# A two-layer hybrid decoder on one core: the second layer's split weights made in the first layer's later blocks

## The chip, the cores and the metric

The kernel runs on 1 core of a Trainium2 chip. The core has a matmul engine (PE, with its weight loads, PEld), VectorE (DVE), ScalarE (ACT), GpSimd (POOL), and SyncE (SP), whose instruction stream issues all DMAs of this kernel, one after the other. Each engine runs its own instructions in order. The metric is the device time of one execution in microseconds (us).

## The reference, cut to what matters

Two layers work on 2048 prompt tokens (and on 64 sample tokens: 8 sequences of 8). One input projection feeds four recurrences, whose outputs are gated, joined and projected; cross-attention into 256 memory tokens follows.

```python
def mixer(h, l, pos, st, v_first, P):
    proj = h @ P['w_in'][l]                       # 1024 -> 3920 columns
    p_ret, p_hgrn, p_gla, p_rwkv = jnp.split(proj, [...], axis=-1)
    ...                                           # four chunked recurrences, each gated with silu(g)
    out = jnp.concatenate([o_ret, o_hgrn, o_gla, o_rwkv], axis=-1) @ P['w_out'][l]

def run_trunk(x, pos0, mem_k, mem_v, init, P):
    for l in range(DEPTH):                        # DEPTH = 2
        out, st_l, v_first = mixer(rmsnorm(x, P['norm_mix'][l]), l, pos, ...)
        x = x + out
        x = x + cross_attend(rmsnorm(x, P['norm_x'][l]), P['wq_x'][l], P['wo_x'][l], mem_k[l], mem_v[l])
```

Everything is float32.

## The kernel before, in words

**Blocks.** The prompt is cut into four blocks of 512 tokens; the program goes through the four blocks of the first layer (A0 to A3 below) and then the four of the second (B0 to B3). A block runs: input projections of RWKV, the RWKV recurrence (`R_rwkv`, four 128-token units on two PSUM lanes), projections and recurrence of GLA, of HGRN and of retention (`R_ret`, two halves), the gates (`gates`), and `finish`, with the output projection `w_out`, the next block's norm (`ahead`, `pre_norm`) and cross-attention. The sample tokens ride along: their projections in block 0, most of their recurrences and their gates in blocks 0 and 1, their output in block 1 (`TURN`).

**Split weights.** A product in float32 is made of three faster ones: weight and activation are each split into a rounded half `hi` and the rest `lo` (type fp32r), and hi.hi, hi.lo and lo.hi are added in PSUM (`dense_c`, `dense_t`). The weights of a layer come in 43 pieces of 128 x 1024 numbers (one is smaller): 31 of `w_in`, 8 of `w_out`, 2 of `wq`, 2 of `wo`. The first time that a piece is needed, which is block 0 of its layer, `parts_of` (line 363) loads the raw piece, ScalarE copies it to `hi` (line 358), GpSimd subtracts to get `lo` (line 359, recorded as L236), and both are stored to DRAM as `parted[key]`; later blocks load the stored pair, 1 MB. `plain` keeps the raw piece as well: the sample tokens' products read it (`wraw`, in float32).

**Buffers.** Raw pieces use the pool `wrp` (3 buffers, tag `w`), pairs the pool `whp` (3 buffers: `whl`). Dense products go to the two PSUM banks `psd`; `psa` and `psc` serve two lanes of the recurrences, `psb` a third.

**What sets the order.** The program is written block by block, and a scheduler then orders each engine's instructions: by priority (the place in the program, shifted by `rank` with the table `PRI`), among those that it takes to be ready by its own estimate of times. So an instruction can stand far from where it is written. At run time each engine keeps that order.

**Names in rows.** `xs` is a normed row block of the next block, transposed on PE (`psb<-fpack,xs`, line 272); `osb` is a recurrence's output in `head_norm` (lines 550 to 569), transposed when its norm is done; `S_ret` and `dn_rv` belong to retention; `th` is a gate's evacuation from `psd` (lines 1265 to 1267); `ol` the `lo` half of a gated output (line 1477).

Of the kernel before, what the change touches and what calls it, by code (L numbers as in the profile page):

```python
# [142 lines left out]
def decoder(ctx, tc, I, C, O):  # L143
# [43 lines left out]
    def right(name):  # L187
        return sided(name, "right")
# [23 lines left out]
    @contextmanager  # L212
    def on_lane(x):
        old, lane[0] = lane[0], x
        yield
        lane[0] = old
# [146 lines left out]
    def parts_of(key, hl, raw, load, plain, again):  # L363


        made = key in parted
        x = None
        if plain or not made:
            x = raw()
            load(x)  # L370
        if made:
            dma(hl.bitcast(F32), parted[key])
        else:
            split_w(x, hl)
            if again:
                parted[key] = drp.tile(list(hl.shape), F32, name="w_" + "_".join(map(str, key)))
                dma(parted[key], hl.bitcast(F32))
        return x

    def load_c(pieces, key, plain, again=True):  # L380

# [890 lines left out]
    def block(l, b, act, hts, st, smp, on, ons, ds, op):  # L1272
# [101 lines left out]
        qk = op.tile([128, 2, TB], F32, name="dn_qk", tag="on_hgrn")  # L1374
        qks = T("ds_qk", [128, 2, SN]) if smp else None
        for i, nm in enumerate(("gla_q", "gla_k")):
            with within("gla", i, 4):
                proj_c(nm, 0, lambda ps: copy_ps(qk[:, i, :], ps), lambda ps: copy_ps(qks[:, i, :], ps))
        gv = op.tile([128, NT, 256], F32, name="dn_gv", tag="on_ret")
        gvs = T("ds_gv", [128, 2, SN]) if smp else None  # L1380
        with within("gla", 2, 4):
            proj_t("gla_v", lambda ps, t0: copy_ps(gv[:, t0:t0 + 2, :], ps), gvs)
        for hb in range(2):
            with within("wk2", hb, 2), on_lane("b"), right("wk2") as wp:
                R_gla(l, pr, st["gla"], dict(qk=h2(qk, hb), v=t2(gv, hb), sm=sm[:, hb * 256:(hb + 1) * 256]), h2(on["gla"], hb), wp)
        if smp:
# [37 lines left out]
        with within("hg", 4, 6):  # L1424
            proj_t("hg_i", lambda ps, t0: copy_ps(hv[:, t0:t0 + 2, :], ps), hvs)
        for hb in range(2):
            with within("wk3", hb, 2), on_lane("b"), right("wk3") as wp:
                R_hgrn(l, pr, st["hgrn"], dict(q=h2(hq, hb), f=h2(hf, hb), v=t2(hv, hb)), h2(on["hgrn"], hb), wp)

# [9 lines left out]
        with within("ret", 2, 3):  # L1439
            proj_t("ret_v", lambda ps, t0: copy_ps(rq["v"][:, t0:t0 + 2, :], ps), rqs["v"])  # L1440
        for hb in range(2):
            with left("wk4") as wp:
                R_ret(l, pr, st["ret"], {nm: t2(rq[nm], hb) for nm in "qkv"}, h2(on["ret"], hb), wp)
        if smp:
# [3 lines left out]
    def gates(l, act, hts, st, smp, on, ons, proj_c, op, wp):  # L1448

        c = cols[l]  # L1450
        hi = [wp.tile([128, 2, 2, TB], F32R, name="oh", tag=f"oh{j}") for j in range(2)]
        oT = [None] * 4
        for nm, cn in (("rwkv", "rw_g"), ("gla", "gla_g"), ("hgrn", "hg_g"), ("ret", "ret_g")):
            h = OKEY.index(nm)
            val = []
            for i in range(2):
                def ev(ps):
                    g = ps
                    if nm == "rwkv":
                        g = dnp.tile([128, TB], F32, name="gs", tag="gs")  # L1460
                        shift_mix(ps, 7 + i, c, st["carry"], g)
                    th = dnp.tile([128, TB], F32, name="th", tag="th", bufs=2)
                    gate_mul(th, g, on[nm][:, i, :], th)
                    A.activation(hi[h // 2][:, h % 2, i, :], th, AF.Copy)
                    val.append(th)

                def evs(ps):
                    g = ps
                    if nm == "rwkv":
                        g = dnp.tile([128, TB], F32, name="gs", tag="gs")[:, :SN]  # L1470
                        shift_mix_s(ps, 7 + i, c, st["shs"], st["ssh"], g)
                    th = dnp.tile([128, SN], F32, name="ths", tag="ths")
                    gate_mul(th, g, ons[nm][:, i, :], ons[nm][:, i, :])
                proj_c(cn, i * 128, ev, evs, smp, hts)
            lo = op.tile([128, 2, TB], F32R, name="ol", tag="on_" + nm)
            for i in range(2):
                tt(V, lo[:, i, :], val[i], hi[h // 2][:, h % 2, i, :].bitcast(F32), ALU.subtract)
            oT[h] = (hi[h // 2][:, h % 2], lo)
        return oT
# [400 lines left out]
        shift_rows(so, O[11][l], SB)  # L1880

    steps = [(l, b) for l in range(depth) for b in range(NB)]
    st = mem = nxt = None
    with on_lane("b"), right("wkn") as wp:
        nxt = []
# [12 lines left out]
    for i, (l, b) in enumerate(steps):  # L1898
        act, hts = nxt
        smp = b == 0  # L1900
        if b == 0:
            ons = {nm: dnp.tile([128, 2, SN], F32, name="ons_" + nm, tag="ons_" + nm) for nm in OKEY}
            ds, hts_l = {}, hts
        fin = b == TURN["end"][l == depth - 1]
        with left("on") as op:
# [9 lines left out]
            rank("D_gate")  # L1915
            oT = gates(l, act, hts_l, st, b == TURN["gate"], on, ons, proj_c, op, wf)
            if b == NB - 1:
                with on_lane("b"), right("wko") as wp:
                    layer_out(l, st, wp)
                    if l + 1 < depth:  # L1920
                        st = layer_state(l + 1, wp)
# [100 lines left out]
```

## Time and profile before

| | us |
|---|---|
| three runs, median (lowest to highest) | 3608.89 (3601.26 to 3626.65) |
| profiled execution, own time | 3606.38 |
| its span, first to last instruction | 3604.6 |
| blocks A1, A2 | 418.1, 427.5 |
| blocks B0, B1, B2 | 518.8, 444.1, 435.4 |

A block is measured from the ScalarE evacuation of its first projection (`sm`, line 536) to that of the next block. Busy times of an engine in a stretch are read against its length; PEclk is the granted clock of PE as a share of the full 2.4 GHz (half of it is the lower level, 1.2 GHz), and its mean over a stretch lies between. In a timeline row the bracket at the end is the time that the engine stood idle before it, and what released it.

### The profile page before, as it was taken

Reading aid. Unit: us, or ns where it says so; the run is one execution under the profiler, and the core shown is the slowest. Engines: PE = TensorE matmul, PEld = TensorE weight load, DVE = VectorE, ACT = ScalarE, POOL = GpSimd, SP = SyncE. Lnnn points to the kernel's source line nnn. Section 1 sums busy time; section 2 is a strip of 40 time slices with the busy share of each in tenths; the row PEclk is TensorE's granted clock in tenths of the full one; section 3 lists DMA queues with packets and bytes.
Section 4 is the critical chain, followed back from the end, with each engine's and each line's share of the span. In section 5 each row is a group of like instructions: output and inputs, shape, how many; then the busy total and the mean of one; then the engine's idle time right before and its main releaser. Section 6 shows DMA issues by size and latency. Waiting matters only on the chain.

```text
span 3604.6 us, 88705 instructions
## 1 busy us (share of the span) xinstructions
PE 3396.8 (94%) x36362; PEld 2817.2 (78%) x36362; DVE 2280.4 (63%) x7543; ACT 1392.1 (39%) x3489; POOL 561.4 (16%) x760
## 2 busy tenths in 40 slices
PE   7999999999999999999999999999889999999998
PEld 5767787777877888788877778778777778877887
DVE  4677645876337754786457865468744677547754
ACT  4452334522244324532445433453214442354323
POOL 3323331020000100110122233101200011000100
PEclk9998999999999999999999999999989999999999
DMA  6432675236652254324542348531554522542254
GB/s 190 151 107 81 187 242 193 72 100 202 212 200 72 100 192 148 113 87 171 180 159 83 103 137 267 172 132 66 160 189 167 170 86 94 193 172 86 73 199 184
DMA packets 244156, 530.92 MB, mean 147 GB/s; under 512 B 66983, under 2 KB 181927, under 8 KB 199719
## 3 DMA queue, kind: packets, MB, share of 16 engines
q1 hardware_dynamic: 243750, 525.25, 42.8%
q8 instruction: 287, 4.70, 0.5%
q14 instruction: 119, 0.97, 0.1%
HBM read 410.04 MB, written 115.16 MB: 146 GB/s over the span
## 4 chain that ended last, share of the span: by engine, by line
PE 73%; DVE 14%; ACT 5%; issue 4%; DMA 2%; POOL 1%; SPq 0%; ACTq 0%; POOLq 0%; DVEq 0%
PE psd L230 40%; PE psc L230 12%; PE psa L230 10%; PE psb L230 5%; PE psc L272 2%; PE psa L272 2%; PE psb L272 2%; DVE rsq L236 1%; DVE Wb L937 1%; DMA wraw<-in_w_in 1%; ACT Xb L939 1%; DVE hri L292 1%; DVE sT L745 1%; DVE hss L561 1%; DVE osb L236 0%
## 5 line engine op out<-in xcount | busy, mean ns | idle before, releaser
L230 PE MATMUL psd<-act,whl 128*128 128x512 f32 (+1 forms) x4032 | 1020.3, 405 | 22.7 <-DVE th L1266 9.6
L230 PEld LDWEIGHTS psd<-act,whl 128*128 128x128 f32 (+1 forms) x4032 | 751.6, 191 | 199.4 <-issue 17.4
L230 PE MATMUL psd<-whl,act 128*128 128x256 f32 x3840 | 544.7, 293 | 5.2 <-POOL whl L236 3.4
L230 PEld LDWEIGHTS psd<-whl,act 128*128 128x128 f32 x3840 | 485.9, 194 | 27.4 <-issue 9.8
L236 POOL TENSOR_TENSOR whl<-wraw,whl 128x1024 fp32r<-128x1024 f32 (+1 forms) x90 | 218.2, 2429 | 335.3 <-ACT whl L358 303.6
L230 PE MATMUL psd<-whl,oh 128*128 128x256 f32 x1152 | 211.6, 284 | 1.2 <-DMA whl<-w_w_out 1.2
L280 POOL TENSOR_TENSOR ri<-ri,mhalf 128x1 f32<-128x1 f32 (+1 forms) x87 | 49.2, 566 | 1039.4 <-DVE ri L279 1005.5
L230 PEld LDWEIGHTS psd<-whl,oh 128*128 128x128 f32 x1152 | 177.5, 189 | 2.6 <-DMA whl<-w_w_out 0.9
L230 PE MATMUL psd<-whl,ol 128*128 128x256 f32 x576 | 162.8, 283 | 0.0
L939 ACT ACTIVATE Xb<-X 32x128 f32<-32x128 f32 x324 | 99.1, 306 | 126.0 <-DVE X L955 78.1
L358 ACT ACTIVATE whl<-wraw 128x1024 fp32r<-128x1024 f32 (+1 forms) x90 | 94.1, 1049 | 124.4 <-PE psa L230 42.4
L745 DVE COPY_PREDICATED sT<-upack,psb 128x128 f32<-128x128 uint8 x320 | 92.6, 326 | 33.1 <-PE psb L230 29.5
L236 DVE TENSOR_TENSOR x<-x,psd 128x256 f32<-128x256 f32 x72 | 30.3, 421 | 128.3 <-PE psd L230 128.3
L230 PEld LDWEIGHTS psd<-whl,ol 128*128 128x128 f32 x576 | 108.6, 189 | 0.4 <-DVE ol L236 0.4
L230 PE MATMUL psb<-dn_hq,dn_hf 64*64 64x32 f32 (+1 forms) x3840 | 99.9, 225 | 7.8 <-DVE dn_hq L236 5.0
L230 PEld LDWEIGHTS psb<-dn_hq,dn_hf 64*64 64x64 f32 x3840 | 82.4, 137 | 31.0 <-issue 17.9
L435 ACT ACTIVATE xs<-xn 128x1024 f32<-128x1024 f32 (+1 forms) x34 | 35.8, 1054 | 155.4 <-PE psb L272 151.2
L1266 DVE SCALAR_TENSOR_TENSOR th<-th,psd 128x512 f32<-128x512 f32 x48 | 32.4, 686 | 91.8 <-ACT th L1265 91.8
L230 PE MATMUL psd<-hts,wraw 128*64 128x64 f32 x1984 | 84.1, 229 | 3.4 <-DVE th L1266 3.4
L230 PEld LDWEIGHTS psd<-hts,wraw 128*64 128x64 f32 x1984 | 69.9, 139 | 21.4 <-issue 11.0
L230 PE MATMUL psa<-whl,oh 128*128 128x256 f32 x448 | 82.8, 283 | 0.0
L230 PE MATMUL psc<-whl,oh 128*128 128x256 f32 x448 | 82.7, 283 | 0.0
(760 smaller groups left out, 7302.3 us busy)
## 6 DMA issues: line engine op xcount, KB each, us to landing
whl<-w_w_out SPq DMA_DIRECT2D x56, 1024.0 KB
wraw<-in_w_in SPq DMA_DIRECT2D x76, 512.0 KB
wraw<-in_w_out SPq DMA_DIRECT2D x32, 512.0 KB
w_w_out<-whl SPq DMA_DIRECT2D x16, 1024.0 KB
x<-x SPq DMA_DIRECT2D x32, 512.0 KB
whl<-w_rw_r SPq DMA_DIRECT2D x12, 1024.0 KB
whl<-w_rw_k SPq DMA_DIRECT2D x12, 1024.0 KB
whl<-w_rw_v SPq DMA_DIRECT2D x12, 1024.0 KB
```

The source lines that it names most:

```text
L230: PE.matmul(out, lhsT=lhsT, rhs=rhs, start=start, stop=stop, skip_group_check=True)
L236: e.tensor_tensor(out, a, b, op)
L272: PE.transpose(out, in_, ident[:rows, :rows])
L280: G.tensor_tensor(y, y, mhalf[:P], ALU.pow)
L292: V.scalar_tensor_tensor(y, t, 1.5, y, ALU.add, ALU.mult)
L358: A.activation(hl[:, 0], raw, AF.Copy)
L435: A.activation(out, xt, AF.Square, accum_out=ss[:P])
L561: V.tensor_reduce(ss[:P, :n4], sq[:P, :n4], AX.X, ALU.add)
L745: V.copy_predicated(out, bc(mk, [P, w, 32 // s, s]), ps)
L937: V.tensor_copy(o, i)
L939: A.activation(o, i, AF.Copy)
L1266: V.scalar_tensor_tensor(th, th, 1.0, x, ALU.add, ALU.mult)
```

## The change

The second layer's 43 pieces are no longer split by `parts_of` in B0. A generator, `prepare(l)`, makes one piece at a time: it loads the raw piece into a `wrp` buffer `lo`, ScalarE copies it to a second `wrp` buffer `hi`, GpSimd subtracts in place, and two DMAs store the halves in DRAM. `some(n)` advances it by n pieces; the calls are written into A1 to A3 (up to 16 pieces in each block: at the GLA projections, before each recurrence half of GLA, HGRN and retention, and at the gates). Since `parted` then holds every key, B0 loads pairs, as the later blocks do, and raw pieces only where the sample tokens need them.

```diff
--- before.py
+++ after.py
@@ -376,6 +376,46 @@
                 parted[key] = drp.tile(list(hl.shape), F32, name="w_" + "_".join(map(str, key)))
                 dma(parted[key], hl.bitcast(F32))
         return x
+
+    def prepare(l):
+
+        w = I["w_in"][l]
+        col = lambda nm, o, n: w[:, OFF[nm] + o:OFF[nm] + o + n]
+        rows = lambda ap: ap.rearrange("(k p) n -> p k n", p=128)
+        half = lambda ap, h: rows(ap[h * 512:(h + 1) * 512])
+        todo = [((l, "low"), [128, 8, 80], [(rows(col(nm, 0, n)), c) for nm, n, c in (("rw_w", 32, 0), ("rw_a", 32, 32), ("gla_l", 16, 64))])]
+        for nm in "rkv":
+            todo += [((l, "rw", nm, i), [128, 8, 128], [(rows(col("rw_" + nm, i * 128, 128)), 0)]) for i in range(2)]
+        tok = lambda nm: [((l, nm, h), [128, 4, 256], [(half(col(nm, 0, 256), h), 0)]) for h in range(2)]
+        ch = lambda nm, n: [((l, nm, o), [128, 8, 128], [(rows(col(nm, o, 128)), 0)]) for o in range(0, n, 128)]
+        todo += ch("gla_q", 128) + ch("gla_k", 128) + tok("gla_v") + ch("hg_f", 256) + ch("hg_q", 256) + tok("hg_i")
+        for nm in ("ret_q", "ret_k", "ret_v"):
+            todo += tok(nm)
+        for nm in ("rw_g", "gla_g", "hg_g", "ret_g"):
+            todo += ch(nm, 256)
+        for q in range(4):
+            todo += [((l, "w_out", q, h), [128, 4, 256], [(half(I["w_out"][l][:, q * 256:(q + 1) * 256], h), 0)]) for h in (1, 0)]
+        todo += [((l, "wq", h), [128, 4, 256], [(half(I["wq_x"][l], h), 0)]) for h in range(2)]
+        todo += [((l, "wo", n), [128, 2, 512], [(rows(I["wo_x"][l][:, n * 512:(n + 1) * 512]), 0)]) for n in range(2)]
+        for key, shape, pieces in todo:
+            lo = wrp.tile(shape, F32R, name="wlo", tag="w")
+            raw = lo.bitcast(F32)
+            for ap, c in pieces:
+                dma(raw[:, :, c:c + ap.shape[2]], ap)
+            hi = wrp.tile(shape, F32R, name="whi", tag="w")
+            A.activation(hi, raw, AF.Copy)
+            tt(G, lo, raw, hi.bitcast(F32), ALU.subtract)
+            parted[key] = drp.tile([128, 2] + shape[1:], F32, name="w_" + "_".join(map(str, key)))
+            for j, x in enumerate((hi, lo)):
+                dma(parted[key][:, j], x.bitcast(F32))
+            yield
+
+    later = [None]
+
+    def some(n):
+        if later[0]:
+            for _ in range(n):
+                next(later[0], None)
 
     def load_c(pieces, key, plain, again=True):
 
@@ -1374,6 +1414,7 @@
         qk = op.tile([128, 2, TB], F32, name="dn_qk", tag="on_hgrn")
         qks = T("ds_qk", [128, 2, SN]) if smp else None
         for i, nm in enumerate(("gla_q", "gla_k")):
+            some(1)
             with within("gla", i, 4):
                 proj_c(nm, 0, lambda ps: copy_ps(qk[:, i, :], ps), lambda ps: copy_ps(qks[:, i, :], ps))
         gv = op.tile([128, NT, 256], F32, name="dn_gv", tag="on_ret")
@@ -1381,6 +1422,7 @@
         with within("gla", 2, 4):
             proj_t("gla_v", lambda ps, t0: copy_ps(gv[:, t0:t0 + 2, :], ps), gvs)
         for hb in range(2):
+            some(2)
             with within("wk2", hb, 2), on_lane("b"), right("wk2") as wp:
                 R_gla(l, pr, st["gla"], dict(qk=h2(qk, hb), v=t2(gv, hb), sm=sm[:, hb * 256:(hb + 1) * 256]), h2(on["gla"], hb), wp)
         if smp:
@@ -1424,6 +1466,7 @@
         with within("hg", 4, 6):
             proj_t("hg_i", lambda ps, t0: copy_ps(hv[:, t0:t0 + 2, :], ps), hvs)
         for hb in range(2):
+            some(2)
             with within("wk3", hb, 2), on_lane("b"), right("wk3") as wp:
                 R_hgrn(l, pr, st["hgrn"], dict(q=h2(hq, hb), f=h2(hf, hb), v=t2(hv, hb)), h2(on["hgrn"], hb), wp)
 
@@ -1439,6 +1482,7 @@
         with within("ret", 2, 3):
             proj_t("ret_v", lambda ps, t0: copy_ps(rq["v"][:, t0:t0 + 2, :], ps), rqs["v"])
         for hb in range(2):
+            some(1)
             with left("wk4") as wp:
                 R_ret(l, pr, st["ret"], {nm: t2(rq[nm], hb) for nm in "qkv"}, h2(on["ret"], hb), wp)
         if smp:
@@ -1453,6 +1497,7 @@
         for nm, cn in (("rwkv", "rw_g"), ("gla", "gla_g"), ("hgrn", "hg_g"), ("ret", "ret_g")):
             h = OKEY.index(nm)
             val = []
+            some(1)
             for i in range(2):
                 def ev(ps):
                     g = ps
@@ -1880,6 +1925,7 @@
         shift_rows(so, O[11][l], SB)
 
     steps = [(l, b) for l in range(depth) for b in range(NB)]
+    ahead_parts = (x for l in range(1, depth) for x in prepare(l))
     st = mem = nxt = None
     with on_lane("b"), right("wkn") as wp:
         nxt = []
@@ -1898,6 +1944,7 @@
     for i, (l, b) in enumerate(steps):
         act, hts = nxt
         smp = b == 0
+        later[0] = ahead_parts if l == 0 and b else None
         if b == 0:
             ons = {nm: dnp.tile([128, 2, SN], F32, name="ons_" + nm, tag="ons_" + nm) for nm in OKEY}
             ds, hts_l = {}, hts
@@ -1915,6 +1962,8 @@
             rank("D_gate")
             oT = gates(l, act, hts_l, st, b == TURN["gate"], on, ons, proj_c, op, wf)
             if b == NB - 1:
+                for _ in ahead_parts if l == 0 else ():
+                    pass
                 with on_lane("b"), right("wko") as wp:
                     layer_out(l, st, wp)
                     if l + 1 < depth:
```

How the engines' orders change. First SP at the end of A0, where the query weights of A0's attention (`wq`) and the first projections of A1 (`w_low`, `w_rw_r`) are loaded. Before:

```order
L233 DMA wraw<-in_w_in 128x8x128
L233 DMA w_wq_6555<-whl 128x2048
L233 DMA wraw<-in_w_in 128x8x128
L233 DMA w_wq_6562<-whl 128x2048
L233 DMA wraw<-in_w_in 128x8x128
L233 DMA whl<-w_low 128x16x80
L233 DMA whl<-w_rw_r_452 128x2048
L233 DMA woraw<-in_wo_x 128x2x512
L233 DMA whl<-w_rw_r_509 128x2048
L233 DMA whl<-w_rw_k_568 128x2048
```

With the change:

```order
L233 DMA w_low<-whi 128x640
L233 DMA w_low<-wlo 128x640
L233 DMA wlo<-in_w_in 128x8x128
L233 DMA w_wq_6562<-whl 128x2048
L233 DMA whl<-w_low 128x16x80
L233 DMA w_rw_r_8796<-whi 128x1024
L233 DMA w_rw_r_8796<-wlo 128x1024
L233 DMA wlo<-in_w_in 128x8x128 x2
L233 DMA w_rw_r_8937<-whi 128x1024
L233 DMA w_rw_r_8937<-wlo 128x1024
L233 DMA wlo<-in_w_in 128x8x128
L233 DMA whl<-w_rw_r_452 128x2048
```

The three raw loads for A1's gates are gone from here; two pieces' raw loads and stores stand ahead of the first r weights of A1, and more follow.

PE at the end of B0, from the last retention products to the output projection (`psd<-act,whl` are gate projections). Before:

```order
L230 MATMUL psd<-act,whl 128x512 x11
L230 MATMUL psc<-S_ret,rqT 64x128 x2
L230 MATMUL psc<-dn_rv,sT 64x64 x4
L230 MATMUL psc<-S_ret,rqT 64x128 x2
L230 MATMUL psc<-dn_rv,sT 64x64 x4
L230 MATMUL psc<-dn_rv,rkd 64x64 x4
L272 MATMUL psb<-fpack,xs 128x128 x12
L272 MATMUL psa<-fpack,osb 128x128 x4
L230 MATMUL psd<-act,whl 128x512 x96
```

With the change:

```order
L230 MATMUL psd<-act,whl 128x512 x9
L230 MATMUL psc<-S_ret,rqT 64x128 x2
L230 MATMUL psc<-dn_rv,sT 64x64 x4
L230 MATMUL psc<-S_ret,rqT 64x128 x2
L230 MATMUL psc<-dn_rv,sT 64x64 x4
L230 MATMUL psc<-dn_rv,rkd 64x64 x4
L230 MATMUL psd<-act,whl 128x512 x36
L272 MATMUL psa<-fpack,osb 128x128 x4
L272 MATMUL psb<-fpack,xs 128x128 x12
L230 MATMUL psd<-act,whl 128x512 x96
```

Thirty-six gate matmuls now stand between the last retention product and the transposes of `osb` and `xs`.

PE at the end of A1, where sample products of the gates (`psd<-hts,wraw`) stand as well. Before:

```order
L230 MATMUL psa<-dn_rv,sT 64x64 x4
L230 MATMUL psa<-dn_rv,rkd 64x64 x4
L230 MATMUL psd<-act,whl 128x512 x12
L230 MATMUL psd<-hts,wraw 64x64 x16
L272 MATMUL psb<-fpack,xs 128x128 x8
L230 MATMUL psd<-act,whl 128x512 x24
L272 MATMUL psc<-fpack,osb 128x128 x4
L272 MATMUL psb<-fpack,xs 128x128 x4
```

With the change:

```order
L230 MATMUL psa<-S_ret,rqT 64x128 x2
L230 MATMUL psa<-dn_rv,sT 64x64 x4
L230 MATMUL psa<-S_ret,rqT 64x128 x2
L230 MATMUL psa<-dn_rv,sT 64x64 x4
L272 MATMUL psb<-fpack,xs 128x128 x4
L272 MATMUL psc<-fpack,osb 128x128 x4
L230 MATMUL psd<-hts,wraw 64x64 x16
L230 MATMUL psd<-act,whl 128x512 x24
```

The gate matmuls that stood between the last retention products and the transpose of `osb` now stand elsewhere: some of them earlier in the block, the others behind it. At the end of B1 the last rows up to `osb` read like these in both kernels; with the change a group of 24 gate matmuls stands there ahead of the first half's `osb`, and none did before:

```order
L272 MATMUL psa<-fpack,dn_rq 128x128 x4
L230 MATMUL psd<-act,whl 128x512 x24
L272 MATMUL psc<-fpack,osb 128x128 x4
L272 MATMUL psc<-fpack,dn_rk 128x128 x4
L272 MATMUL psb<-fpack,xs 128x128 x6
```

That is how the changed kernel has it, in A1 and in B1 alike. The order of A3, B2 and B3 is the same in both kernels but for a few rows; all 43 copies stand between the end of A0 and the middle of A2.

## Rows read from the trace of the kernel before

**Rows 1.** The page: span; busy us (share), instructions of each engine.

```profile
span 3604.6 us, 88705 instructions
PE 3396.8 (94%) x36362; PEld 2817.2 (78%) x36362; DVE 2280.4 (63%) x7543; ACT 1392.1 (39%) x3489; POOL 561.4 (16%) x760
```

**Rows 2.** Windows, blocks A1, A2, B0, B1, B2: length, busy (instructions), PEclk, DMA, GB/s.

```profile
548.30:966.40 418.10, 402.41 (x4543) 334.82 (x4542) 272.92 (x952) 149.84 (x395) 50.12 (x85) 0.99 0.46 153
966.40:1393.90 427.50, 417.35 (x4310) 344.64 (x4307) 252.99 (x877) 162.56 (x413) 32.30 (x71) 1.00 0.41 143
...
1770.30:2289.10 518.80, 477.41 (x5199) 390.38 (x5198) 335.73 (x1023) 219.90 (x518) 145.62 (x130) 0.96 0.46 152
2289.10:2733.20 444.10, 412.89 (x4575) 342.97 (x4574) 286.08 (x972) 157.29 (x415) 52.68 (x89) 0.97 0.44 145
2733.20:3168.60 435.40, 424.72 (x4341) 350.65 (x4339) 267.88 (x898) 171.47 (x435) 35.36 (x76) 0.99 0.40 139
```

**Rows 3.** Groups of B0: count, busy us, mean ns; idle before them, releasers.

```profile
L236 POOL TENSOR_TENSOR whl<-wraw,whl 128x1024 fp32r<-128x1024 f32 x40 | 98.3, 2457 | 163.1 <-ACT whl L358 134.7 <-PE psa L272 14.2 <-PE psc L230 13.3
...
L358 ACT ACTIVATE whl<-wraw 128x1024 fp32r<-128x1024 f32 x40 | 42.3, 1056 | 54.8 <-PE psa L230 20.7 <-DMA wraw<-in_w_in 17.4 <-PE psd L230 8.2
```

**Rows 4.** Waits of PE in B0: who, for whom, us in total, times, longest.

```profile
PE psd L230 <- POOL whl L236: 2.1, 3, 1.2
```

**Rows 5.** Timeline, end of B0 (start, us, [idle before]), one A1 piece, two windows.

```profile
895.53 5.61 PE L230 MATMUL psd<-act,whl 128*128 128x512 f32 x24
...
2184.34 1.09 PE L272 MATMUL psb<-fpack,xs 128*128 128x128 f32 x4 [4.37 <-DVE xs L439]
...
2187.88 1.09 PE L272 MATMUL psa<-fpack,osb 128*128 128x128 f32 x4 [2.46 <-DVE osb L236]
...
2190.86 21.35 PE L230 MATMUL psd<-act,whl 128*128 128x512 f32 x81 [1.90 <-DVE th L1266]
...
2170.00:2190.00 20.00, 12.14 (x108) 9.21 (x108) 11.21 (x35) 5.42 (x10) 5.07 (x3) 0.82 0.82 263
2190.00:2210.00 20.00, 19.14 (x72) 15.63 (x73) 12.50 (x13) 7.00 (x11) 5.35 (x2) 0.83 0.54 194
```

**Rows 6.** Timeline and windows, end of B1.

```profile
2607.76 0.60 ACT L636 ACTIVATE osb<-psa 128x512 f32<-128x512 f32 x1 [3.31 <-PE psa L230]
...
2615.22 1.09 PE L272 MATMUL psb<-fpack,xs 128*128 128x128 f32 x4 [5.86 <-DVE xs L439]
...
2617.55 1.11 PE L272 MATMUL psc<-fpack,osb 128*128 128x128 f32 x4 [1.25 <-DVE osb L236]
...
2620.21 1.43 PE L230 MATMUL psc<-rqT,rkT 64*128 64x128 f32 x5 [0.69 <-ACT rkT L865]
...
2634.16 1.09 PE L272 MATMUL psc<-fpack,osb 128*128 128x128 f32 x4 [6.83 <-DVE osb L236]
...
2637.14 1.98 PE L230 MATMUL psd<-hts,wraw 128*64 128x64 f32 x32 [1.90 <-DVE th L1266]
...
2610.00:2630.00 20.00, 10.18 (x92) 9.05 (x92) 12.20 (x36) 3.73 (x7) 2.15 (x3) 0.66 0.11 38
2630.00:2650.00 20.00, 13.62 (x106) 11.09 (x107) 11.34 (x28) 6.62 (x13) 0.00 (x0) 0.74 0.61 202
```

**Rows 7.** Timeline of B0: one VectorE pair alone, and one beside a GpSimd subtraction.

```profile
2192.72 1.29 DVE L236 TENSOR_TENSOR ol<-th,oh 128x512 fp32r<-128x512 f32 x2
...
2206.45 2.67 POOL L236 TENSOR_TENSOR whl<-wraw,whl 128x1024 fp32r<-128x1024 f32 x1 [2.82 <-ACT whl L358]
...
2206.91 3.37 DVE L236 TENSOR_TENSOR ol<-th,oh 128x512 fp32r<-128x512 f32 x2
```

**Rows 8.** Timeline and a window, end of A1.

```profile
869.31 0.60 PE L272 MATMUL psc<-fpack,osb 128*128 128x128 f32 x4
...
871.80 1.15 PE L230 MATMUL psd<-hts,wraw 128*64 128x64 f32 x32 [1.46 <-DVE th L1266]
...
868.00:888.00 20.00, 17.83 (x162) 14.39 (x161) 9.49 (x19) 6.05 (x12) 0.00 (x0) 1.00 0.97 310
```

## The prediction

> Block names: A0 to A3 are the first layer's four blocks of 512 tokens, B0 to B3 the second's. Times of places in the trace are those of the run before.
>
> **What bounds the kernel now.** The page's busy times come first [rows 1]: the matmul engine (PE) is busy 3396.8 of 3604.6 us, no other engine over 65%. So a gain has to come out of the 208 us in which PE is idle, or out of PE's own low clock, and work moved between other engines is worth nothing by itself. Then the same view cut at the blocks [rows 2] (a block starts where the evacuation of its first projection starts): PE is idle 15.7 us in A1, 10.1 in A2, but 41.4 in B0 (518.8 - 477.4), 31.2 in B1 and 10.7 in B2, and the granted clock is 0.96 in B0 and 0.97 in B1 against 0.99 to 1.00. B0 is the block whose splitting leaves, and the worst of the five. The groups of B0 [rows 3] give what leaves it: 40 ScalarE copies (42.3 us) and 40 GpSimd subtractions (98.3 us); two smaller groups complete the 43 pieces. And the waits of B0 [rows 4] warn: PE waits directly for a subtraction 2.1 us in all. The rest of the 41 us is waits for VectorE and ScalarE chains, which the splitting can only have lengthened or put in a bad order. The order at the ends of blocks (previous section) is therefore half of the argument.
>
> **The change part by part.** The sum is made against the profiled execution, 3606.4 us (span 3604.6 and 1.8 around it), which lies 2.5 us under the median of the runs, 3608.9.
>
> *Amounts.* 43 pieces, each a load of the raw weights, a copy, a subtraction and two stores, leave B0 (there: one store of both halves) and stand, by the order, all between the end of A0 and the middle of A2; none is left for A3. B0 then loads 43 ready pieces, and still the raw ones of 23 (its sample projections read them). The SP queue grows by 111 DMAs, traffic by some 55 MB (43 ready loads of 1 MB, 23 raw loads of 0.5 MB) on 531; at B0's 152 GB/s [rows 2] this is no bound by itself, since the blocks that get it are at 143 to 153 GB/s and A1 holds stretches of 310 [rows 8].
>
> *End of B0: -13.* PE waits 4.37, 2.46 and 1.90 us here for the next block's norm, for the last retention norm and for a gate's evacuation [rows 5], 8.7 in all, and the clock is 0.82 and 0.83 in the 40 us around it: the 81 matmuls from 2190.86 take 21.35 where 24 at full clock take 5.61 [rows 5], so 18.9, 2.4 lost, and about 2 more in the 20 us before. In the new order 36 dense matmuls (36/24 of 5.61, 8.4 us) stand between the last state update and these transposes, so the norms finish under them. 8.7 + 4.4 = 13. Ends: 0 (the waits turn up behind the 36) and -13.
>
> *Rest of B0: -13.* Without the 8.7 B0 is idle 32.7; at B2's rate (10.7 in 435.4) it would be 12.7 of 518.8. The surplus of 20 is shared between the splitting and the sample recurrences that B2 has not got and that stay. I take two thirds, because 2.1 us are waits for subtractions outright and because ScalarE loses 54.8 us of idle time ahead of copies in its own order, 17.4 of it for raw weights to land [rows 3], which holds up evacuations behind them. Ends: 0 and -31, all of the surplus and the rest of the clock (0.96 against 0.99 is 15 us of 519, 4.4 of them used above).
>
> *End of A1: +14.* The order here gets worse. Now the last retention transpose of A1 has no wait and the sample matmul behind it 1.46 [rows 8], because dense matmuls stand between; in the new order there are none, and the rows read like the end of B1 in the kernel before. That end shows the price [rows 6]: waits of 5.86, 1.25, 0.69, 6.83 and 1.90 (16.5), clock 0.66 and 0.74 in 40 us; 32 sample matmuls take 1.98 against 1.15 [rows 6, 8]; I put the loss over the 40 us at 3, by analogy with the 4.4 at the end of B0. Of the waits the 6.83 and 1.90 return in full. The first norm's chain, 9.8 us from 2607.76 to 2617.55, now has 24 dense matmuls and one transpose group ahead, 6.2, so 3.6 remain. 8.7 + 3.6 + 3 - 1.46 = 14. Ends: 0 and +20 (all five waits and the clock).
>
> *End of B1: -5.* The same 24 dense matmuls now stand there too: 7.8 us of waits (5.86 + 1.25 + 0.69) become 3.6, and a us of clock. The 6.83 stays. Ends: -10 and 0.
>
> *The pieces in their new place: +10.* Nobody waits for their results, but they use engines that others wait for. What a subtraction does to VectorE stands in two rows [rows 7]: the same pair of VectorE subtractions takes 1.29 us alone and 3.37 when a GpSimd subtraction of 2.67 runs beside it. So a hit costs 2.1. VectorE is busy 65% of A1 and 59% of A2 [rows 2]; with 6 in 10 hit, 43 pieces lengthen it by 54 us. PE pays part of that: in B0 at most 20 (the surplus) of a like amount, and there it waited for the halves themselves. I take a fifth, 10, with ScalarE's waits for landings in it. Ends: 0 (A1 and A2 have idle VectorE time) and +90 (every piece hits and PE pays all). The Trainium skill, page "SBUF — State Buffer", section "SBUF: two separate sides", says that a VectorE instruction with two SBUF operands and a GpSimd one that reads SBUF take a shared port pair as an exclusive lock, the loser blocked for the whole instruction. By that rule the hits move with the pieces and none is saved; the two rows agree, 2.1 more beside 2.67.
>
> Sum: -13 - 13 + 14 - 5 + 10 = -7, so 3606.4 - 7 = **3599 us**. Even if all is as supposed, what B0 gives is nearly taken by A1 and A2, which are the blocks with the least idle time.
>
> **Rivals.**
> *The lock decides (slower).* VectorE's lengthened operations lie in the recurrences of A1 and A2, where PE has few dense matmuls left to put between. Then PE pays all 54: -17 + 54 = +37, 3643. It is slower than before as soon as PE pays over 17 of the 54, about a third. For it: PE idles only 10 to 16 us in A1 and A2, so there is order but little slack. Against it: B0 carried the same hits and was not 54 us worse than B2. Chance 0.12. The rule of the Trainium skill named above (page "SBUF — State Buffer", section "SBUF: two separate sides") speaks for this case: each hit would cost up to a whole subtraction.
>
> *Weights come late in A1 (no gain).* SP is one queue in order. Two pieces' stores now stand ahead of the first r weights of A1; each waits for a raw load (ScalarE's waits average 17.4/12 = 1.5 and reach 5.6 us), a copy of 1.06 and a subtraction of 2.46. That is up to 9.1 a piece, 18 us, and at A1's gates four pieces share the queue where DMA is at 0.97 for 20 us [rows 8]. +20 on the forecast: 3619. For it: raw weights for A1's gates were loaded a block ahead, and their buffers now hold pieces. Against: PE works on A0's attention meanwhile. Chance 0.12.
>
> *The new order does not hurt (faster).* If A1's end finds its norms finished anyway, and PE pays nothing for the hits, then -13 - 20 - 5 = -38: 3568. For it: the largest cost I set is read from another block. Against: the rows of the two ends are alike. Chance 0.18.
>
> My forecast has 0.58. That the change does not do what it says is out: the order shows the copies gone from B0.
>
> **The numbers.** 1% of the median, 36 us, is what a measurement of this kernel can tell from no change: faster is under 3573, slower over 3645. Faster: 0.7 of the last rival and a 25th of the forecast, 0.15. Slower: 0.6 of the first and little of the second, 0.08. Same: 0.77. The range from 3566 to 3636 holds the forecast with most of its terms' ends, the late weights, the good order down to its own number, and the lock up to half its price; some 2 in 10 lie outside.
>
> **What would show it.** B0 shorter by 20 to 30 us with its idle time near 20 and clock 0.98; no waits over 2 us before its last transposes. A1 longer by 10 to 20, with a wait of 6 to 7 for the last retention norm and a clock under 0.8 behind it. A2 longer by less than 10, VectorE busier there by some 30 us and in B0 less by as much. B1 shorter by about 5; A3, B2, B3 as now, since their order is the same. I am wrong if A1's end has no such wait, if A2 grows by over 15, or if PE in A1 waits for weights.

## The result, and the profile after

| | this | before, beside it | ratio [95%] |
|---|---|---|---|
| median us (lowest to highest) | 3627.39 (3616.66 to 3641.8) | 3608.53 (3599.32 to 3626.65) | 1.0054 [1.0041, 1.0066] |

The change makes the kernel slower, by about half a per cent. That lies inside the stated range and inside "within 1%", but 3599 had the wrong sign. The profiled execution took 3616.66 us with a span of 3614.9, against 3604.6 [rows 1]: 10.3 us to be found in the traces. It is the shortest of the 16 runs; the medians lie 18.9 us apart, and what makes up the other 8.6 no trace here shows.

The page of the kernel after, first lines (busy us, share, instructions):

```profile
span 3614.9 us, 88867 instructions
...
PE 3392.8 (94%) x36362; PEld 2820.1 (78%) x36362; DVE 2293.9 (63%) x7543; ACT 1395.6 (39%) x3489; POOL 560.5 (16%) x760
```

The totals are those of before. The windows cut at the blocks, A1, A2, B0, B1 and B2 of the kernel after (columns as in [rows 2]), are not:

```profile
543.80:984.30 440.50, 410.10 (x4544) 342.44 (x4544) 285.37 (x952) 162.57 (x408) 79.63 (x97) 0.97 0.58 194
984.30:1447.40 463.10, 430.35 (x4309) 353.65 (x4307) 292.69 (x876) 189.33 (x440) 96.86 (x98) 0.97 0.65 223
...
1826.00:2307.30 481.30, 461.56 (x5186) 380.62 (x5184) 294.45 (x1017) 178.50 (x473) 49.77 (x90) 0.99 0.43 145
2307.30:2748.10 440.80, 414.03 (x4575) 344.69 (x4576) 284.03 (x972) 156.28 (x414) 46.53 (x87) 0.97 0.43 143
2748.10:3182.00 433.90, 423.17 (x4341) 349.73 (x4339) 267.76 (x898) 171.61 (x435) 35.33 (x76) 1.00 0.40 139
```

Against [rows 2]: B0 37.5 shorter, A1 22.4 longer, A2 35.6 longer, B1 3.3 shorter; A0, A3, B2 and B3 together 6 shorter. A2 is where the forecast breaks. VectorE executes as many instructions there as before (876 and 877) and is busy 292.69 us instead of 252.99. PE is idle 32.75 us (463.10 - 430.35) instead of 10.15, and busy 13.0 us longer for the same matmuls, at a granted clock of 0.97 instead of 1.00: the 35.6 us are 22.6 of idle time and 13.0 of clock. The groups of A2 after, GpSimd's pieces and then one VectorE line (count | busy us, mean ns):

```profile
L236 POOL TENSOR_TENSOR wlo<-wlo,whi 128x1024 fp32r<-128x1024 f32 x27 | 64.5, 2390 | 131.0 <-ACT whi L406 130.0 <-DMA wlo<-in_w_in 0.9
```
```profile
L284 DVE TENSOR_SCALAR rsq<-hss 128x8 f32<-128x8 f32 (+1 forms) x10 | 5.1, 507 | 0.2
```

27 subtractions run in A2, and a VectorE operation on 4 or 8 columns, some 0.17 us alone, takes 0.51 on average. One such hit in the timeline of A2 (start, us, engine, operation; `hri` and `rsq` are the steps of a reciprocal root, one after the other):

```profile
1164.11 0.14 DVE L236 TENSOR_TENSOR rsq<-rsq,hri 128x4 f32<-128x4 f32 x1
1164.24 2.37 POOL L236 TENSOR_TENSOR wlo<-wlo,whi 128x1024 fp32r<-128x1024 f32 x1 [3.19 <-ACT whi L406]
1164.29 0.29 DVE L673 SCALAR_TENSOR_TENSOR S_gla<-S_gla,tot,psb 64x64 f32<-64x64 f32 x1
1164.60 2.03 DVE L292 SCALAR_TENSOR_TENSOR hri<-rsq,hri 128x4 f32<-128x4 f32 x1
...
1167.55 0.15 DVE L292 SCALAR_TENSOR_TENSOR hri<-rsq,hri 128x4 f32<-128x4 f32 x1
...
1167.76 0.42 DVE L236 TENSOR_TENSOR wosb<-wosb,hri 128x256 f32<-128x256 f32 x1
...
1168.23 0.69 PE L272 MATMUL psa<-fpack,wosb 128*128 128x128 f32 x2 [2.08 <-DVE wosb L236]
```

A step of 0.15 us takes 2.03: it ends when the subtraction that started at 1164.24 ends. The 2 us go down the chain to the norm of `wosb`, and PE waits 2.08 for it. From here on the **stretch** of a block is the sum of this: each VectorE instruction against the median of its form in both traces, what those more than 0.15 us over it have too much (a form is operation and operand shapes; drawn wider or narrower, it moves the sums by up to 4 us in A1 and A2 and up to 9 in A0 and B0). In A2 it is 2.6 us before (6 instructions) and 40.4 after (37); in A1 7.3 and 18.7; in B0 42.8 and 9.6; in A0, which splits its own weights in both kernels, 47.6 and 50.8. Counted in the timeline of A2, 22 of the 27 subtractions each hold one VectorE operation. PE waits over 0.6 us 17 times there (25.4 us in all), and 13 of these waits (19.5 us) come within 3 us of the end of a subtraction; before, there were three such waits in A2 (4.6 us).

A1's end reads as forecast. Timeline and two windows of 20 us there, after:

```profile
868.09 1.11 PE L272 MATMUL psc<-fpack,osb 128*128 128x128 f32 x4 [3.08 <-DVE osb L236]
...
877.43 0.66 PE L272 MATMUL psb<-fpack,xs 128*128 128x128 f32 x4 [0.93 <-DVE xs L479]
...
884.17 1.08 PE L272 MATMUL psc<-fpack,osb 128*128 128x128 f32 x4 [6.09 <-DVE osb L236]
...
887.15 1.97 PE L230 MATMUL psd<-hts,wraw 128*64 128x64 f32 x32 [1.90 <-DVE th L1306]
```
```profile
864.00:884.00 20.00, 10.08 (x105) 8.42 (x103) 14.35 (x44) 4.61 (x8) 2.63 (x4) 0.85 0.47 157
884.00:904.00 20.00, 17.60 (x146) 14.21 (x148) 8.27 (x17) 6.78 (x12) 2.40 (x1) 0.81 0.77 246
```

The first half's norm is waited for 3.08 us, the last retention norm 6.09 and the gate behind it 1.90, where [rows 8] had none for the last norm and 1.46 for the gate, and the granted clock falls to 0.81 behind PE's idle 10 us.

### The profile page after: what moved, and what is told of

It reads as the page before. It is cut to its first block, busy times and chain, and to the rows that moved or that the text cites. A ratio compares the mean times of both kernels' runs of the same rounds, so it can differ in the third digit from the quotient of the medians.

```text
span 3614.9 us, 88867 instructions
## 1 busy us (share of the span) xinstructions
PE 3392.8 (94%) x36362; PEld 2820.1 (78%) x36362; DVE 2293.9 (63%) x7543; ACT 1395.6 (39%) x3489; POOL 560.5 (16%) x760
## 4 chain that ended last, share of the span: by engine, by line
PE 69%; DVE 17%; ACT 5%; DMA 3%; issue 3%; POOL 2%; SPq 0%; ACTq 0%; POOLq 0%; DVEq 0%
PE psd L230 37%; PE psc L230 12%; PE psa L230 10%; PE psb L230 5%; PE psc L272 2%; PE psa L272 2%; PE psb L272 2%; DVE rsq L236 1%; DVE Wb L977 1%; DVE osb L236 1%; DVE qx L236 1%; DVE hri L292 1%; ACT Xb L979 1%; DVE hss L601 1%; DVE Xb L977 1%
## 5 line engine op out<-in xcount | busy, mean ns | idle before, releaser
L236 POOL TENSOR_TENSOR whl<-wraw,whl 128x1024 fp32r<-128x1024 f32 (+1 forms) x49 | 118.3, 2420 | 155.2 <-ACT whl L358 143.2
L236 POOL TENSOR_TENSOR wlo<-wlo,whi 128x1024 fp32r<-128x1024 f32 (+1 forms) x43 | 102.0, 2372 | 235.4 <-ACT whi L406 234.4
```

What stands on the lines that cost most here:

```text
L236: e.tensor_tensor(out, a, b, op)
```

## The experiments

Two theories about A2 and A1. **The port:** a GpSimd subtraction holds up VectorE operations in the recurrences and PE pays. **Order and load:** the pieces' transfers, copies and changed order cost it. All edits but e5's are to the kernel after or, where said, to an earlier experiment. Each edit also makes the scheduler order the blocks anew, so a row differs from another by more than its edit. How far a length can be read is seen where the order is the same but for a few rows: the eleven kernels with the changed order of B1 have it at 434.0 to 447.6 (granted clock 0.96 to 0.99), the three with the old order of A1 (before, e7, e8) all at 418.1 to 418.3. Block lengths in us from each profiled execution, one for each kernel, cut as above:

| | A0 | A1 | A2 | A3 | B0 | B1 | span | ratio to before [95%] |
|---|---|---|---|---|---|---|---|---|
| before | 511.5 | 418.1 | 427.5 | 376.4 | 518.8 | 444.1 | 3604.6 | |
| after | 507.5 | 440.5 | 463.1 | 378.6 | 481.3 | 440.8 | 3614.9 | 1.0054 [1.0041, 1.0066] |
| e1 no subtraction | 507.2 | 437.6 | 432.9 | 380.5 | 485.6 | 447.2 | 3596.1 | 0.9958 [0.9940, 0.9976] |
| e2 memsets | 504.6 | 429.1 | 443.1 | 378.6 | 485.2 | 445.0 | 3591.1 | 0.9972 [0.9958, 0.9986] |
| e3 on VectorE | 512.4 | 441.6 | 435.5 | 378.1 | 482.5 | 434.0 | 3592.4 | 0.9966 [0.9944, 0.9988] |
| e4 DMAs only | 509.8 | 424.6 | 430.8 | 380.4 | 485.1 | 443.4 | 3581.3 | 0.9914 [0.9891, 0.9938] |
| e5 before, VectorE | 481.5 | 423.3 | 427.3 | 377.7 | 502.2 | 451.3 | 3569.0 | 0.9888 [0.9864, 0.9913] |
| e6 all on VectorE | 480.3 | 438.3 | 436.3 | 380.0 | 482.4 | 441.4 | 3567.3 | 0.9886 [0.9848, 0.9924] |
| e7 late, VectorE | 509.1 | 418.3 | 440.7 | 377.4 | 482.7 | 440.7 | 3575.5 | 0.9902 [0.9873, 0.9930] |
| e8 late, GpSimd | 510.4 | 418.2 | 468.6 | 384.6 | 482.1 | 441.5 | 3609.9 | 1.0007 [0.9989, 1.0026] |
| e9 late, all on VectorE | 483.8 | 423.0 | 440.7 | 377.2 | 481.9 | 447.3 | 3558.1 | 0.9842 [0.9813, 0.9870] |
| e10 at A1's gates | 483.2 | 458.4 | 439.0 | 377.8 | 482.2 | 447.6 | 3591.9 | 0.9960 [0.9946, 0.9975] |
| e11 copies on GpSimd | 481.0 | 423.2 | 456.7 | 377.8 | 486.0 | 437.1 | 3568.8 | 0.9882 [0.9863, 0.9902] |

### e1 to e4: what of a piece costs

e1:
```diff
-            tt(G, lo, raw, hi.bitcast(F32), ALU.subtract)
```


> The change without its 43 GpSimd subtractions: the raw piece is stored as the second half (the split is left incomplete). Lock theory: A2 and A1 pay for VectorE operations that wait for those subtractions (VectorE time in A2 253 to 293 us, about the growth of the block, 428 to 463). Without them VectorE in A2 falls to 255 to 260, A2 to 427 to 435, the kernel to about 3580 (ratio to before 0.990 to 0.994). Queue theory (ScalarE copies and SP stores wait in order for landings and hold up what is behind them): A2 stays over 450, ratio 1.002 to 1.006. Order theory (the scheduler's new order of A1 and A2 is worse by itself): A2 over 450 with VectorE near 255.

e2:
```diff
-            tt(G, lo, raw, hi.bitcast(F32), ALU.subtract)
+            for _ in range(2):
+                G.memset(raw, 0.0)
```


> Each of the 43 subtractions is replaced by two GpSimd memsets of the same tile (the second half stored is zero): GpSimd is busy at the same places, but reads nothing from SBUF. Lock theory, with the lock between operand reads: VectorE time in A2 255 to 260, A2 427 to 435, ratio 0.990 to 0.994, like the kernel without subtractions. GpSimd-queue theory (short GpSimd operations of the recurrences and norms stand behind the long ones): A2 over 450, ratio 1.002 to 1.006, VectorE in A2 near 255. If a memset locks as well, A2 stays over 450 with VectorE at 285 or more.

e3:
```diff
-            tt(G, lo, raw, hi.bitcast(F32), ALU.subtract)
+            tt(V, lo, raw, hi.bitcast(F32), ALU.subtract)
```


> The 43 subtractions on VectorE, where one of 128x1024 takes 1.22 us when alone: 52 us of VectorE time in place of the some 49 us that VectorE operations lose to the lock. Lock theory, with VectorE's time as what A1 and A2 pay for: A2 about 460, ratio 1.003 to 1.008, as the change. Queue theory: the same. If VectorE's own time is cheaper than being held up at a bad moment, 0.996 to 1.002.

e4:
```diff
-            hi = wrp.tile(shape, F32R, name="whi", tag="w")
-            A.activation(hi, raw, AF.Copy)
-            tt(G, lo, raw, hi.bitcast(F32), ALU.subtract)
...
-            for j, x in enumerate((hi, lo)):
+            for j, x in enumerate((lo, lo)):
```


> The pieces without copy and subtraction: the raw piece is loaded and stored twice (both halves are the raw numbers), so only the DMAs and their places on SP are left, and ScalarE's 43 copies are gone too. Lock theory: hardly better than without the subtraction, ratio 0.989 to 0.994, A2 427 to 433. Queue theory with ScalarE: far better than the kernel that keeps the copies, by 20 us or more. Queue theory with SP and DMA alone: A2 over 450.

Measured: without the subtractions (e1) A2 is 432.9 (stretch 3.1), with them on VectorE (e3) 435.5 (stretch 5.1). The total of e1, 0.9958, misses the 0.990 to 0.994 expected, because A1 stays long; that of e3, 0.9966, lies in the last branch of its expectation. The window of A2 and the group of e3 show that it is not VectorE's load:

```profile
990.80:1426.30 435.50, 422.08 (x4309) 347.96 (x4307) 286.05 (x903) 187.49 (x441) 36.23 (x71) 0.99 0.70 237
```
```profile
L236 DVE TENSOR_TENSOR wlo<-wlo,whi 128x1024 fp32r<-128x1024 f32 x27 | 33.8, 1252 | 4.9 <-ACT whi L406 4.7
```

VectorE is busy 286.05 us, with 27 instructions more, against 292.69 after; yet the block is 27.6 shorter. The same busy us, as instructions where VectorE had nothing to do, leave the block 8 over before; as stretch inside chains they leave it 36 over. For A2 the port theory holds. For A1 it does not: 437.6, 441.6 and 440.5 with none, VectorE's and GpSimd's subtractions; of the 12 subtractions in A1 seven hold an operation, and three of these are followed by a PE wait over 0.6 us within 3 us. The DMAs alone (e4) leave A1 6.5 longer than before and A2 3.3. In A1 most of this is order: e4 has PE's order of e5 there, where no piece stands in A1 and the block takes 423.3 against 424.6, so the transfers of 12 pieces cost about 1 us. e1, which adds the copies, has 13 more in A1 and 2 in A2, and its total is 13 us above e4's: more than the "hardly better" of the one theory and less than the 20 of ScalarE's queue. e2's A1 is 429.1 with the same 12 copies in another order, so the copies' time alone does not set the loss; how much is order and how much copies is not shown.

The memsets separate two kinds of VectorE operation. Two stretches of A2 of e2 (timeline):

```profile
1088.39 1.97 POOL L408 MEMSET wlo<- 128x1024 f32 x2 [8.67 <-ACT whi L406]
1088.45 0.42 DVE L236 TENSOR_TENSOR kp<-kp,EA 128x256 f32<-128x256 f32 x1
1088.79 0.16 DVE L236 TENSOR_TENSOR rsq<-rsq,rn 128x4 f32<-128x4 f32 x1
1088.86 0.16 DVE L292 SCALAR_TENSOR_TENSOR rn<-rsq,rn 128x4 f32<-128x4 f32 x1
...
1194.24 2.09 DVE L978 COPY Xb<-X 32x128 f32<-32x128 f32 x2
1194.29 1.96 POOL L408 MEMSET wlo<- 128x1024 f32 x2 [11.21 <-ACT whi L406]
```

Operations with two SBUF inputs run at their usual 0.16 and 0.42 beside a memset; a copy from SBUF to SBUF is held (two take 2.09; the same copy takes 0.22 on average in A2 of the kernel before). So e2 lies between the branches of its expectation: A2 443.1 with VectorE busy 268.41 us and a stretch of 19, half of what the subtractions gave.

### e5 and e6: what the port cost before

e5, edited from the kernel before:
```diff
-    def split_w(raw, hl, e=G):
+    def split_w(raw, hl, e=V):
```


> The kernel before with its own subtraction of each weight part (split_w) on VectorE instead of GpSimd; nothing is moved. It asks what the 85 stretched VectorE operations of A0 and B0 cost the kernel before (47.6 us more than their median in A0, 42.8 in B0). 'The shared port decides': A0 falls from 511.5 to 475 to 495 and B0 from 518.8 to 485 to 500, though VectorE gets 40 subtractions more in each (about 1.2 us each); the total is 3550 to 3585. 'VectorE's load decides, wherever it comes from': 40 x 1.2 = 48 us of subtractions take the place of 45 us of stretch, A0 and B0 stay within 8 us of before, the total within 15 of 3605. A1, A2, A3, B1 to B3 as before in both.

e6, edited from the kernel after:
```diff
-    def split_w(raw, hl, e=G):
+    def split_w(raw, hl, e=V):
...
-            tt(G, lo, raw, hi.bitcast(F32), ALU.subtract)
+            tt(V, lo, raw, hi.bitcast(F32), ALU.subtract)
```


> The change with every subtraction of weight parts on VectorE, the 40 of A0 and the 42 of the later blocks. Against the version with only the moved ones on VectorE (A0 512.5, A1 441.6, A2 435.5, B0 482.4) only A0 should differ. 'The shared port decides': A0 475 to 495, total 3560 to 3580. 'VectorE's load decides': A0 505 to 520, total 3585 to 3605.

Measured: one default argument changed in the kernel before makes it 1.1% faster. A0 of the kernel before and of e5 (windows):

```profile
36.80:548.30 511.50, 470.27 (x5145) 388.58 (x5145) 325.43 (x980) 200.58 (x457) 161.47 (x134) 0.94 0.48 158
```
```profile
34.60:516.10 481.50, 449.90 (x5145) 374.76 (x5145) 330.10 (x1031) 202.65 (x459) 51.53 (x87) 0.98 0.51 167
```

VectorE does 51 instructions more and is busier by 4.7 us, and A0 is 30 us shorter. B0 falls by 16.6 to 502.2, just above the 485 to 500 expected; its remaining 20 above 482 is what making the pieces there costs without the port, with the order at B0's end in it. A1 and B1 were expected as before and are 5.2 and 7.2 longer: A1 has another order, B1 the old one at a clock of 0.94 against 0.97. e6's A0 confirms the 30: the five kernels with these subtractions on VectorE have A0 at 480.3 to 483.8, the eight with them on GpSimd at 504.6 to 512.4. The order of A0 changes with the engine as well. Beside e5, e6 shows what the move brings once the port is out of it: 0.9886 and 0.9888, nothing that can be measured: B0's 20 and B1's 10 (which is within what B1 scatters) go into A1 (15) and A2 (9).

### e7, e8 and e9: pieces from A2 on

e7, edited from e3; e8, from the kernel after; e9 has this line and e6's two:
```diff
-        later[0] = ahead_parts if l == 0 and b else None
+        later[0] = ahead_parts if l == 0 and b > 1 else None
```


> The change with the moved subtractions on VectorE, and the pieces made from A2 on only (35 in A2, 7 in A3, none in A0 and A1). It takes A1's order back to that of before. 'The new order of A1 costs': A1 returns from 441.6 to 415 to 422, A2 goes from 435.5 to 438 to 450 (nine pieces more), A3 378 to 384, total 3570 to 3585. Rival 'what A1 loses is the pieces' own load and moves with them': A1 418, but A2 455 or more, total as with the pieces in A1 (3590 to 3600).

> The change as it is (subtractions on GpSimd), the pieces made from A2 on only (35 in A2, 7 in A3). 'The shared port costs in A2 by the hit': A2 was 463.2 with 26 pieces against 432.9 without subtractions, 1.15 us a piece, so 35 pieces give 433 + 40 = 473 (465 to 482), A3 380 to 392, A1 415 to 422; total 3595 to 3620. 'A2's loss is the order of the pieces, not the port': A2 within 8 us of the same order with VectorE subtractions (the run beside it).

> The two remedies together: the pieces made from A2 on only, and every subtraction of weight parts on VectorE. If the two act apart, A0 is 480 to 482 as with all subtractions on VectorE, A1 415 to 424, A2 441 to 445, A3 377 to 380, B0 480 to 485, B1 to B3 as in the runs before, and the total is the one of the late version, 3575.5, less the 29 to 32 of A0: 3540 to 3555, a ratio to before of 0.98 to 0.985. If part of A0's gain is given back in A1 (A1 was 423.3 after the faster A0 of the kernel before with its subtractions on VectorE), it is 3550 to 3562.

Measured: A1 returns to 418.3 and 418.2, with VectorE's and ScalarE's instructions there in the sequence of the kernel before; eight pieces more (35) cost A2 5 us on VectorE. On GpSimd the same program has A2 at 468.6, 27.9 longer, with a stretch of 39.3 against 5.1. The order inside A2 is not the same: 563 of VectorE's 876 other instructions stand in the same sequence in e7 and e8. But A2 lies at 427.3 to 440.7 in four different orders whose stretch is at most 7, and at 463.1 and 468.6 in the one order of the kernel after and e8, with 40; e2 and e11, with 19 and 16, lie between at 443.1 and 456.7. So A2's length goes with the held operations over seven orders; that the order which GpSimd's subtractions bring costs nothing of its own is not shown apart. (By the hit I expected 473; the price per piece fell a little.) e9 is the fastest version, 1.6% under before. It came out at 3556.08, above the 3540 to 3555 of two remedies that act apart and within the 3550 to 3562 named for the other case: A1 is 423.0 and not 418, as in e5, and VectorE's instructions there stand in e5's sequence, another than before's. A changed A0 changes A1's order even with no piece in it.

### e10: pieces only at A1's gates

Edited from e6 (the other calls outside the gates likewise; `gate_only[0] = b == 1` is set ahead of each block):
```diff
-            some(2)
+            some(0 if gate_only[0] else 2)
...
-            some(1)
+            some(3 if gate_only[0] else 1)
```


> All subtractions on VectorE; the pieces that A1's calls make are asked for at A1's gates (three at each of four calls) and none in its recurrences; the program's order puts 3 at A0's end, 8 late in A1, 29 in A2. 'What A1 loses is the order of its recurrences when pieces stand among them': A1 falls from 438.3 to 418 to 428, A2 436 to 446. 'Pieces anywhere in A1 cost it its 20 us' (their transfers and copies, not their place): A1 432 to 442.

Measured: neither; A1 is 458.4, the worst of all. The waits of PE in A1 and of the DMA queue from 818 to 920 us, its end (us in total, times, longest), and the timeline of the queue:

```profile
PE psd L230 <- DMA wraw<-in_w_in: 24.5, 3, 19.9
```
```profile
SPq L233 <- ACT whi L406: 32.5, 7, 7.9
```
```profile
869.07 0.32 SPq L233 DMA_DIRECT2D w_gla_k<-whi  x1
870.33 0.32 SPq L233 DMA_DIRECT2D w_gla_k<-wlo  x1
870.74 1.50 SPq L233 DMA_DIRECT2D wraw<-in_w_in  x2
...
876.00 1.97 PE L230 MATMUL psd<-hts,wraw 128*64 128x64 f32 x32 [19.94 <-DMA wraw<-in_w_in]
```

The raw weights that A1's sample gates need stand in SP's queue behind the stores of pieces, which wait for their copies: 24.5 us of PE's waits, where A1 is 20.1 longer than in e6. This is the rival of late weights, which the change itself did not show (its PE waits for ready weights in A1 are 0.9 and 0.3 us) and this placement does.

### e11: copies on GpSimd

Edited from e9:
```diff
-            A.activation(hi, raw, AF.Copy)
+            G.tensor_copy(hi, raw)
```


> Pieces from A2 on only, subtractions on VectorE, and the 42 copies of the moved pieces (the rounded high part) on GpSimd instead of ScalarE: a GpSimd operation that reads one input and writes one. 'Any GpSimd operation that reads and writes here holds VectorE': the stretch of VectorE in A2 rises from 5 us to 25 or more and A2 from 441 to 455 to 470. 'Only the two-input subtraction does it': stretch below 10, A2 436 to 444, since ScalarE has 37 us less to do there. Against the same version with copies on ScalarE the total is 10 to 30 longer in the first case, the same or up to 6 shorter in the second.

Measured: A2 456.7 and the total 13.9 above e9's, in the ranges of the first theory, but the stretch is 16.3 and not 25. A GpSimd copy, 1.07 us on average, does hold a VectorE step with two SBUF inputs (timeline of A2; the step takes some 0.16 alone):

```profile
1137.16 1.04 POOL L406 CAST whi<-wlo 128x1024 fp32r<-128x1024 f32 x1 [5.64 <-DVE wlo L236]
1137.21 1.01 DVE L292 SCALAR_TENSOR_TENSOR hri<-rsq,hri 128x4 f32<-128x4 f32 x1
```

So it is not the two-input subtraction alone that holds VectorE; each hold is shorter, as the copy is. There is another wait as well (VectorE's group in A2, its idle time last):

```profile
L236 DVE TENSOR_TENSOR wlo<-wlo,whi 128x1024 fp32r<-128x1024 f32 (+1 forms) x37 | 44.7, 1209 | 22.7 <-POOL whi L406 22.6
```

VectorE stands 22.6 us in its own order for copies that are not ready. How A2's 16 us over e9 divide between the two is not separated here.

## Why the prediction was wrong, step by step

| step | forecast | profile |
|---|---|---|
| End and rest of B0 | -26 | -37.5 |
| End of A1 | +14 | +15 |
| End of B1 | -5 | -3.3 |
| The pieces in their new place | +10 | +36 in A2, +7 in the rest of A1 |
| blocks not named, and the start | 0 | -7 |
| sum | -7 | +10 |

**The step that failed is "The pieces in their new place: +10", and in it the sentence "PE pays part of that ... I take a fifth".** The sum of the hits was about right: 54 us of VectorE were forecast, the stretch of A1 and A2 grew by 49 (in A2 more hits than forecast, 22 of 27, each shorter, 1.5 us on average). How much PE pays was not. In A2 e3 puts it at 28 of 35 (27.6 us of length for a stretch of 40.4 against 5.1), and e1 at 30: four fifths instead of one, and over half of the 49. The term also had no clock in it, where "End of A1" had: of the 27.6 us, 19.3 are PE's idle time and 8.3 are matmuls that run longer, at 0.97 against 0.99. A2's other 8 are the pieces' copies, transfers and subtractions as such. The rival "The lock decides", at chance 0.12, is what A2 shows. Its 3643 was too high because A1's hits cost nothing that e3 shows and B0 gave 11 us more; for the same reason its break-even of 17 us was too low, 26 with the ends of A1 and B1 and B0 as measured. That the time still lies inside the range is partly luck: 11.5 us of B0 and 7 of blocks not named, which nothing forecast, went against the 33 that the pieces cost more.

The fifth was taken from B0, and B0 was a bad measure of A2. Its own price was near what the prediction allowed ("at most 20"): e5 takes 16.6 us off it for its 42.8 of stretch, two fifths, and 30 off A0 for 47.6. To halve that and carry it to A2 had no row behind it. A0's long idle time (41.2 us) stood in the trace and I did not look at it, because the change does not touch it. It was the second reading of the same price. In B0 of the kernel before 8 of 22 held operations are followed within 3 us by a PE wait over 0.6 us, in A2 of the kernel after 12 of 22, as at 1168.23: there the hits fall among serial steps of 0.15 us in the recurrences.

The Trainium skill, page "SBUF — State Buffer", section "Who interferes with whom", adds to the lock cited in the prediction that VectorE copies and tensor-scalar operations can enter a two-port mode and then contend with GpSimd, while operations with two SBUF inputs contend only with a GpSimd one that reads SBUF. The rows of e2 agree: memsets hold the copy (2.09 for two) and not the two-input operations (0.16). I had priced a pair of two-input operations alone.

**B0** gave more than forecast. Its idle time fell from 41.4 to 19.7 as said (near 20), and the clock is 0.99. But "no waits over 2 us before its last transposes" did not come true, since one wait for the next norm is left, 3.51 us where there were 8.7 in three (kernel after):

```profile
2211.79 0.63 PE L272 MATMUL psb<-fpack,xs 128*128 128x128 f32 x4 [3.51 <-DVE xs L479]
```

So the end gave less of its waits than forecast and the rest of B0 more. PE's busy time also fell, 477.41 to 461.56: 15.8 us, where I had counted 4.4 of clock and kept the rest as an end of the range.

**A1's end** was right in mechanism and size: in the two windows shown PE is idle 12.3 us, where it was 2.2 over the same part of the block before, and at 0.85 and 0.81 it loses some 10.08 x 0.15 + 17.6 x 0.19 = 4.9; together 15 more. e7 and e8 show that it belongs to the pieces in A0 and A1: without them A1 is back within 0.2 us, and in its old order. Of the whole 22 in A1, the transfers of the pieces are about 1 by e4 and e5, and order alone can cost 5 (e5, with another A0 and no pieces). The rest, order and copies together, stays open, as e1, e2 and e3 each change the order too.

**B1** has 0.93 where it waited 5.86 for the next norm, and 6.10 for the 6.83 [rows 6], as said (kernel after):

```profile
2641.28 0.66 PE L272 MATMUL psb<-fpack,xs 128*128 128x128 f32 x4 [0.93 <-DVE xs L479]
...
2648.04 1.08 PE L272 MATMUL psc<-fpack,osb 128*128 128x128 f32 x4 [6.10 <-DVE osb L236]
```

Its 3.3 us are less than the 13.6 by which B1 scatters in one order, so the size is not shown. Weights were not late in A1. Of the signs named beforehand, "A2 grows by over 15" came true against me.

## What to carry to other kernels

GpSimd work is not free to VectorE: look in the trace for short VectorE operations that end where a GpSimd operation ends, and price them in the chain they stand in, with the clock that PE loses by its waits, not by VectorE's share of busy time. Before such work is moved, read what it costs in every block that has it now: here one changed engine brought more than the move. And a DMA queue in order makes a load wait for whatever the stores ahead of it wait for, so stores that wait belong where no load is urgent.

## What was not expected of the hardware

In A2 of the kernel after, 76 VectorE instructions ran more than 0.1 us beside a piece's subtraction; 22 were stretched, nearly by the whole overlap (2.37 us beside 2.54 for the longest chain step), and none of these reads PSUM, transposes or reduces. The subtraction takes 2390 ns on GpSimd and 1252 on VectorE. The 98.3 us of GpSimd time in B0 [rows 3] were dearer than the 50 us on VectorE (40 x 1252 ns) that they saved: with the subtractions on VectorE (e5) B0 is 16.6 us shorter.
